# First norm on ScalarE, early up weights and token differences on VectorE alone, in a two-layer hybrid decoder step

## The chip, the cores and the metric

The kernel runs on one core of one Trainium2 chip. The time is the device time of one execution in microseconds, the median over several runs.

## The reference

One inference step of a two-layer decoder for a prompt of 1024 tokens and a sample group of 8 x 8 tokens, 1088 tokens in all, model width 1024, in float32. Layer 0 mixes tokens by two state-space heads, layer 1 by latent attention over a paged cache. Both layers end in the same way; this is what the change touches:

```python
def layer_norm(x, g, b):
    mu = jnp.mean(x, -1, keepdims=True)
    var = jnp.mean(jnp.square(x - mu), -1, keepdims=True)
    return (x - mu) * lax.rsqrt(var + EPS) * g + b

def conv_ffn(x, buf, w_up, conv_w, conv_b, w_down):      # d_ff 2816, both halves 5632 columns
    h = x @ w_up
    h, new_buf = causal_dwconv(h, buf, conv_w, conv_b)   # depthwise, width 3
    return (silu(h[..., :D_FF]) * h[..., D_FF:]) @ w_down, new_buf

x = layer_norm(ALPHA * x + mixer(x), ln1_g, ln1_b)       # mixer ends in an output projection
x = layer_norm(ALPHA * x + conv_ffn(x), ln2_g, ln2_b)
```

## The kernel before

A float32 product is made of three passes of a reduced float format, hi x hi, hi x lo and lo x hi (`mm3`, L207-213). So every operand is split: ScalarE casts it to hi, VectorE subtracts hi from it for lo (`split` L218, `lo` L216, `load_split` L222-226 for weights that come through a raw buffer, where another engine can be named for the subtraction). Tokens lie in nine tiles (eight of 128, one of 64). SBUF is divided by hand into fields A to H whose space passes from one stage to the next. The order of instructions on each engine is set by a scheduler from the program's order and from which buffers are free; a generator's `yield` marks where a caller may put other work.

The stages of a layer, with their place in the trace of layer 0 and of layer 1:

- **Output projection and first norm**, `out_ln` (L1519-1578), 424 to 530 and 2236 to 2322. Two halves of 512 columns. In the second half each finished token tile is added to the residual, normalised by `ln` (L234-246: statistics on VectorE, square root on ScalarE, reciprocal, then two VectorE passes of 128x1024 with the gain and bias rows broadcast over the partitions), stored to `xm` in DRAM, and turned by eight TensorE transposes (`to_raw`, L261-272), which ScalarE copies from PSUM into `XT`, one half of the tokens each.
- **Up-projection**, first part of `ffn` (L276-437), to about 1040 and 2840. 22 blocks of columns. Within one, seven products P1 to P7 in the manner of Strassen stand for eight block products, for each half u of the tokens; a product is 12 matmuls of 272 columns, a block 168. The products need differences of weight quarters (`sums` L326-331 on GpSimd, S4 at L337) and of token quarters (`tokens` L296-315: per half eleven differences and lo parts, 128x1088, at L301, of which three run on GpSimd, and seven casts at L304). Block 0 runs u = 0 first, then u = 1; the raw weights of block 1 go into the space that `XT` leaves.
- **Down-projection**, second part of `ffn` (L439-548), to about 1300 and 3097. Three passes over the tokens (three tiles each), each with 22 steps: `fetch` loads one row block of `w_dn` and the activations of the step, through a ring of two raw weight buffers `wr` and four split ones `wd`. At steps 14 to 16 the residual rows come back from `xm` (`residual` L499-502), after the last step `finish` (L479) adds the products, and `norm` does the second norm in the next pass.
- **Input projection of layer 1**, `in1` (L1605 on), behind the third pass. Its weights come in eight pieces of 128x704 through two raw buffers of their own, split by ScalarE and GpSimd.

Of the kernel before, what the change touches and what calls it, by code (L numbers as in the profile page):

```python
# [113 lines left out]
class Net:  # L114
# [132 lines left out]

    def to_T(self, x, M, x_, c0):
# [12 lines left out]
    def to_raw(self, x, M, XT, c0):  # L261

        nc = self.nc
        for a in range(0, 8, 4):
            t = self.ps("tr")
            for j in range(4):
                nc.tensor.transpose(t[:, j * M : (j + 1) * M], x[:, (a + j) * P : (a + j + 1) * P], self.ident[:M, :M])
            tv = t[:, : 4 * M].rearrange("p (k m) -> p k m", k=4)
            for u in range(2):
                lo, hi = max(c0, u * HT), min(c0 + M, u * HT + HT)  # L270
                if lo < hi:
                    nc.scalar.copy(XT[u][:, a : a + 4, lo - u * HT : hi - u * HT], tv[:, :, lo - c0 : hi - c0])


    def ffn(self, i, XT, gt, src, dst, fields):

        nc, A = self.nc, self.A
        V, G = nc.vector, nc.gpsimd  # L280
        gp, gw, gr, gs, gc, ge, gx = (self.group() for _ in range(7))
        cpar, stt, ffp = gp("F^", 2 * NBLK, 4), gp("F^", 2 * NBLK, NB, 2), gp("F^", 2 * NBLK, 2)
# [4 lines left out]
        X = {}  # L287
        for p, g, fl in (("P1", gc, "C"), ("P6", gc, "C"), ("P2", ge, "E"), *((p, gx, fields) for p in ("P5", "P7", "P4", "P3"))):
            X[p] = [g(fl, 2, 4, QT) for _ in range(2)]
        W = {p: [gs("HEC", 4 * P) for _ in range(2)] for p in PRODUCTS}  # L290
        raws = [gw("F", 2 * D)]
# [4 lines left out]
        def tokens(u):  # L296

            x = XT[u]
            B11, B21 = x[:, :4, :QT], x[:, 4:, :QT]
            B12, B22 = x[:, :4, QT:], x[:, 4:, QT:]  # L300
            sub = lambda eng, o, a, b: eng.tensor_tensor(o, a, b, op=ALU.subtract)  # L301

            def parts(p, full, eng=V):
                nc.scalar.copy(X[p][u][:, 0], full)  # L304
                sub(eng, X[p][u][:, 1], full, X[p][u][:, 0])


            parts("P1", B11)
            parts("P2", B21)
            sub(V, B11, B12, B11)  # L310
            sub(G, B12, B22, B12)
            parts("P3", B22, G)
            sub(V, B22, B22, B11)
            sub(V, B21, B21, B22)
            parts("P6", B22)
            parts("P5", B11)
            parts("P7", B12, G)
            parts("P4", B21)


        def load(blk):
            raw = raws[blk % len(raws)]
            for half in range(2):
                nc.sync.dma_start(raw[:, half * D : half * D + D], A["w_up"][i, half * NBLK + blk])

        def sums(blk):  # L326
            raw = raws[blk % len(raws)]
            A11, A12, A21, A22 = (raw[:, k * 512 : k * 512 + 512] for k in range(4))
# [72 lines left out]
        load(0)  # L401
        sums(0)
        for p in first:
            weights(p)
# [15 lines left out]
        for blk in range(NBLK):  # L420
            if blk + 1 < NBLK:
                load(blk + 1)
# [19 lines left out]
        ar = [gl("F", 384) for _ in range(3)]  # L442
        wr = [gl("F", D) for _ in range(2)]
# [55 lines left out]
        def residual(b, j):  # L499
            t = groups[b][j]  # L500
            M = min(P, NT - t * P)
            nc.sync.dma_start(res[j][:M], src[rows(t), :])
# [9 lines left out]
        x_ = yield  # L512
        self.epoch("H", F32)
        gb = self.load_ln(g, "H", "ln2", i)
        res = [g("HF", D) for _ in range(3)]
        todo = [(b, k) for b in range(3) for k in range(NBLK)]
        late = []
        for n, (b, k) in enumerate(todo):
# [66 lines left out]
def arrange(x):  # L585
# [35 lines left out]
    for k in ("ln1_g", "ln1_b", "ln2_g", "ln2_b"):  # L621
        a[k] = lay(x[k])
    a["w_up"] = lay(x["ffn_w_up"].reshape(2, 8, P, 44, P).transpose(0, 3, 2, 1, 4).reshape(2, 44, P, D))
# [54 lines left out]
class Layer0(Net):  # L678
# [840 lines left out]
    def out_ln(self, name, i, m_, XT, res, src, dst, ks=range(8), rows=None):  # L1519
# [38 lines left out]
        gb = self.load_ln(g, "F^", "ln1", i)  # L1558
        self.epoch("H", F32R)
        xs = self.stack(g("H", 2, 4, P), m_)  # L1560
        for nh in range(2):
            if nh:
                for n in range(8):
                    weights(1, n)
            for tt in self.token_tiles if nh else range(4, NTT):
# [7 lines left out]
                if nh:  # L1573
                    x = res[:M, tt, :]
                    self.ln(x, M, gb, f"a{i}_{tt}")
                    nc.sync.dma_start(dst[tt * P : tt * P + M, :], x)
                    self.to_raw(x, M, XT, tt * P)
# [6 lines left out]
class Layer1(Layer0):  # L1584
# [19 lines left out]
    def in1(self, x_):  # L1604
# [4 lines left out]
        gw = self.group()  # L1609
        raws = [gw("F", 2, 352) for _ in range(2)]  # L1610
# [7 lines left out]
        gw.free()  # L1618
        yield
# [738 lines left out]
    def run(self):  # L2358
# [9 lines left out]
        for _ in self.out_ln("w_out0", 0, m_, XT, res, A["x_tok"], xm[0]):  # L2368
# [5 lines left out]
        xs = self.dp.tile([NT, D], F32, tag="xs", name="xs")  # L2374
        ffn = self.ffn(0, XT, gt, xm[0], xs, "BD")
# [4 lines left out]
        ffn.send(x_)  # L2380
        self.places()
        rest = self.in1(x_)
        next(rest)
# [14 lines left out]
        out = []  # L2398

        def then():  # L2400
# [13 lines left out]
            out.extend((m_, XT, self.out_ln("w_out1", 1, m_, XT, res, xs, xm[1], heads, rows)))  # L2414
# [20 lines left out]
        ffn = self.ffn(1, XT, gd, xm[1], A["o_y"], "AB")  # L2435
        next(ffn)
        ffn.send(None)
# [25 lines left out]
```

## Time and profile before

| | |
|---|---|
| median of 3 runs | 3106.66 us (3103.35 to 3110.38) |
| profiled execution | 3098.84 us, of which the span is 3097.1 us |
| instructions in the span | 51653 |
| mean granted TensorE clock | 0.975 of full speed |
| moved by DMA | 356.32 MB, 115 GB/s on the mean |

The page gives the busy time of each engine over the whole span, which says little of a single stage. For that, the trace is asked in four ways: the waits of an engine, each with the instruction that ended it; windows, that is the busy time of every engine within a stretch, with the granted TensorE clock (1.00 is 2.4 GHz, 0.50 is 1.2 GHz) and the load of the DMA engines; timelines, instruction by instruction; and the issues of DMAs with the time to their landing. Times in a row are microseconds from the span's start.

### The profile page before, as it was taken

How to read it: one execution, taken by the hardware profiler on the slowest of the kernel's cores; microseconds unless marked ns; L12 is line 12 of the kernel's file. 1: busy time of each engine (PE TensorE's matmuls, PEld its weight loads, DVE VectorE, ACT ScalarE, POOL GpSimd, SP SyncE). 2: the span in 40 equal slices, each digit the busy share in tenths (PEclk: the TensorE clock that was granted, in tenths of full speed). 3: DMA queues.
4: the chain of work that ended last, by engine and by line, in shares of the span. 5: the costliest groups of instructions: out<-in, count | busy, mean ns of one | idle time of the engine just before them, and what ended most of it. 6: DMA issues, size and time to landing. Idle time of an engine off the chain costs nothing.

```text
span 3097.1 us, 51653 instructions
## 1 busy us (share of the span) xinstructions
PE 2967.7 (96%) x19503; PEld 2685.6 (87%) x19503; DVE 2370.2 (77%) x4066; ACT 1554.6 (50%) x2733; POOL 1345.9 (43%) x1299
## 2 busy tenths in 40 slices
PE   8999998799999999999999999999996999999998
PEld 7888786799999888798998888888875999999887
DVE  8753647888989666547667999999768988987665
ACT  3434632444444443345555888888524444444432
POOL 2652521666666100101112999989306666662000
PEclk9999899899999999999999999999997999999999
DMA  3223132222222666510103444444621222225664
GB/s 141 73 54 119 52 124 87 71 70 83 77 71 77 205 214 208 157 46 24 32 28 101 167 160 152 170 171 170 207 86 61 81 74 77 81 69 189 215 207 152
DMA packets 145150, 356.32 MB, mean 115 GB/s; under 512 B 27469, under 2 KB 82957, under 8 KB 136709
## 3 DMA queue, kind: packets, MB, share of 16 engines
q1 hardware_dynamic: 133600, 267.99, 27.1%
q0 software_dynamic: 9216, 83.89, 7.6%
q8 instruction: 154, 2.52, 0.3%
q10 hardware_dynamic: 2084, 1.14, 0.1%
q14 instruction: 96, 0.78, 0.1%
HBM read 293.67 MB, written 58.11 MB: 114 GB/s over the span
## 4 chain that ended last, share of the span: by engine, by line
PE 78%; DVE 13%; ACT 4%; DMA 2%; issue 2%; POOL 2%; ACTq 0%; DVEq 0%; SPq 0%; POOLq 0%
PE ps L211 21%; PE ps L213 21%; PE ps L212 21%; DVE fieldH L2221 2%; PE ps L2277 2%; PE ps L2167 2%; DVE fieldD L216 1%; PE ps L2200 1%; PE ps L471 1%; DVE fieldF L2243 1%; DVE fieldB L216 1%; PE ps L1956 1%; PE ps L2181 1%; PE ps L1925 1%; PE ps L1922 1%
## 5 line engine op out<-in xcount | busy, mean ns | idle before, releaser
L212 PE MATMUL ps<-fieldB,fieldE 128*128 128x272 f32 (+4 forms) x960 | 301.1, 314 | 0.1
L211 PE MATMUL ps<-fieldC,fieldE 128*128 128x512 f32 (+2 forms) x740 | 286.3, 387 | 0.0
L213 PE MATMUL ps<-fieldC,fieldE 128*128 128x512 f32 (+2 forms) x740 | 285.9, 386 | 0.0
L212 PE MATMUL ps<-fieldC,fieldE 128*128 128x512 f32 (+2 forms) x740 | 285.7, 386 | 0.0
L216 DVE TENSOR_TENSOR fieldE<-fieldF,fieldE 128x512 fp32r<-128x512 f32 (+4 forms) x265 | 157.1, 608 | 110.7 <-ACT fieldE L456 103.4
L226 DVE TENSOR_TENSOR fieldC<-fieldF,fieldC 128x1024 fp32r<-128x1024 f32 x132 | 162.3, 1230 | 100.5 <-ACT fieldC L225 100.1
L211 PE MATMUL ps<-fieldC,fieldH 128*128 128x272 f32 x704 | 206.5, 293 | 11.8 <-ACT fieldC L304 11.7
L212 PE MATMUL ps<-fieldC,fieldH 128*128 128x272 f32 x704 | 205.0, 291 | 4.9 <-DVE fieldC L301 4.9
L213 PE MATMUL ps<-fieldC,fieldH 128*128 128x272 f32 x704 | 205.3, 292 | 0.0
L225 ACT CAST fieldC<-fieldF 128x1024 fp32r<-128x1024 f32 x132 | 138.5, 1049 | 106.1 <-PE ps L471 56.2
L211 PE MATMUL ps<-fieldA,fieldE 128*128 128x362 f32 (+4 forms) x560 | 180.7, 324 | 7.6 <-ACT fieldA L878 7.3
L212 PEld LDWEIGHTS ps<-fieldB,fieldE 128*128 128x128 f32 x960 | 185.4, 193 | 2.0 <-DVE fieldB L879 0.5
L213 PE MATMUL ps<-fieldA,fieldE 128*128 128x362 f32 (+4 forms) x560 | 182.0, 325 | 0.0
L211 PE MATMUL ps<-fieldB,fieldE 128*128 128x272 f32 (+2 forms) x576 | 171.7, 299 | 2.5 <-DVE fieldD L358 2.5
L213 PE MATMUL ps<-fieldB,fieldE 128*128 128x272 f32 (+2 forms) x576 | 170.6, 296 | 0.0
L213 PEld LDWEIGHTS ps<-fieldC,fieldE 128*128 128x128 f32 x740 | 138.9, 188 | 28.2 <-DVE fieldE L216 0.4
L212 PEld LDWEIGHTS ps<-fieldC,fieldE 128*128 128x128 f32 x740 | 138.8, 188 | 27.4
L211 PEld LDWEIGHTS ps<-fieldC,fieldE 128*128 128x128 f32 x740 | 139.0, 188 | 26.9
L380 DVE SCALAR_TENSOR_TENSOR fieldA<-fieldA,fieldF 128x544 f32<-128x544 f32 (+1 forms) x176 | 145.8, 866 | 21.4 <-ACT fieldA L378 21.4
L380 DVE SCALAR_TENSOR_TENSOR fieldD<-fieldD,fieldF 128x544 f32<-128x544 f32 (+1 forms) x176 | 144.8, 861 | 21.4 <-ACT fieldD L378 21.3
L456 ACT CAST fieldE<-fieldF 128x384 fp32r<-128x384 f32 (+1 forms) x132 | 65.1, 495 | 185.7 <-PE ps L212 160.8
L216 DVE TENSOR_TENSOR fieldD<-ps,fieldE 128x1024 fp32r<-128x1024 f32 x128 | 153.9, 1210 | 1.7 <-ACT fieldE L2171 1.5
(702 smaller groups left out, 10299.7 us busy)
## 6 DMA issues: line engine op xcount, KB each, us to landing
fieldF<-w_dn SPq DMA_DIRECT2D x132, 512.0 KB, 3.6
fieldF<-w_up SPq DMA_DIRECT2D x44, 512.0 KB, 3.6
fieldF<-act SPq DMA_DIRECT2D x88, 192.0 KB, 2.9
fieldA<-w_up SPq DMA_DIRECT2D x22, 512.0 KB, 3.6
fieldD<-w_up SPq DMA_DIRECT2D x22, 512.0 KB, 3.5
fieldF<-w_in SPq DMA_DIRECT2D x16, 512.0 KB, 4.2
fieldF<-w_out SPq DMA_DIRECT2D x32, 256.0 KB, 3.0
xm<-fieldC SPq DMA_DIRECT2D x16, 512.0 KB, 2.6
```

The lines of the kernel that those rows point to most:

```text
L211: mm(out, wh, xh, start=first, stop=False, **kw)
L212: mm(out, wh, xl, start=False, stop=False, **kw)
L213: mm(out, wl, xh, start=False, stop=last, **kw)
L216: self.nc.vector.tensor_tensor(out, full, hi, op=ALU.subtract)
L225: self.nc.scalar.copy(hi, raw)
L226: (eng or self.nc.vector).tensor_tensor(lo, raw, hi, op=ALU.subtract)
L380: V.scalar_tensor_tensor(y[:, :n], x[:, tap : tap + n], c(tap), y[:, :n], op0=ALU.mult, op1=ALU.add)
L456: nc.scalar.copy(a[:, :N], raw)
L471: nc.tensor.matmul(ps, a[:, 256 : 256 + P], w[:, s, cs], start=k + s == 0, stop=k + s == NBLK)
L2167: nc.tensor.transpose(ps[:, t * P : t * P + P], raws[i % 4][:, c : c + P], self.ident)
L2221: V.tensor_tensor_reduce(o, ps[H], o, op0=ALU.add, op1=ALU.max, accum_out=out[H], scale=1.0, scalar=first)
L2277: nc.tensor.matmul(o, x, y, start=t + s == 0, stop=t + s == (8 if J < 8 else 1))
```

## The change

**Norm.** In `out_ln`, `ln` becomes `ln_hat`: the statistics as before, then one VectorE operation on 128x1 and one ScalarE activation over 128x1024 give x̂, the row without gain and bias. x̂ is what `xm` now holds. `to_raw` applies gain and bias where they are per-partition columns, while it copies the transposed blocks: eight activations of 128x128 with scale and bias in place of two copies of 128x512 (columns come from a new small array `ln1_T`). The down-projection's `residual` makes ALPHA·(x̂·g + b) by two VectorE passes, and `finish` adds without a factor. The field with gain and bias rows in the down-projection is loaded anew by `gains`, with ln1 rows at step 12 of each pass and ln2 rows for the second norm.

**Up weights.** `ffn` is a generator whose first part now runs inside `out_ln`, behind the split of the second half's weights: it loads block 0, splits three quarters and makes the four sums on VectorE. The other four products' weights are split behind `out_ln`.

**Token differences.** All 22 are on VectorE.

**Input projection.** The eight weight pieces are loaded at the odd steps 1 to 15 of the third pass of layer 0's down-projection, through `wr`, lo on VectorE.

```diff
+    def ln_hat(self, x, M, tag):
...
+        V.tensor_scalar(mv[:M, 0:1], mv[:M, 0:1], rs[:M], -1.0, op0=ALU.mult, op1=ALU.mult)
+        nc.scalar.activation(x, x, AF.Identity, bias=mv[:M, 0:1], scale=rs[:M])
...
-    def to_raw(self, x, M, XT, c0):
+    def to_raw(self, x, M, XT, c0, gb):
...
-                    nc.scalar.copy(XT[u][:, a : a + 4, lo - u * HT : hi - u * HT], tv[:, :, lo - c0 : hi - c0])
+                        nc.scalar.activation(o, v, AF.Identity, bias=gb[:, 1, k : k + 1], scale=gb[:, 0, k : k + 1])
...
     def ffn(self, i, XT, gt, src, dst, fields):
...
+        raws = [gw("F^", 2 * D)]
+        A11, A12, A21, A22 = load(0)
+        for p, full in (("P1", A11), ("P2", A12), ("P4", A22)):
+            W[p] = [gs("H", 4 * P) for _ in range(2)]
+            self.split(*W[p], full)
+        for o, a, b, op in ((A11, A11, A21, ALU.subtract), (A21, A21, A22, ALU.add), (A22, A22, A11, ALU.subtract), (A12, A12, A22, ALU.subtract)):
+            V.tensor_tensor(o, a, b, op=op)
+        left0 = dict(S1=A21, S2=A22, S3=A11, S4=A12)
+        yield
...
-            sub(G, B12, B22, B12)
-            parts("P3", B22, G)
+            sub(B12, B22, B12)
+            parts("P3", B22)
...
-        load(0)
-        sums(0)
-        for p in first:
-            weights(p)
+        for p in ("P6", "P5", "P7", "P3"):
+            self.split(*W[p], left0[PRODUCTS[p][0]])
         tokens(0)
...
-                V.scalar_tensor_tensor(v, v, ALPHA, ps[:M], op0=ALU.mult, op1=ALU.add)
+                V.tensor_tensor(v, v, ps[:M], op=ALU.add)
...
+            V.scalar_tensor_tensor(x, x, ALPHA, gb[:M, 0], op0=ALU.mult, op1=ALU.mult)
+            V.scalar_tensor_tensor(x, gb[:M, 1], ALPHA, x, op0=ALU.mult, op1=ALU.add)
+
+        def gains(which):
+            for k, n in enumerate("gb"):
+                nc.sync.dma_start(gb[:, k], A[f"{which}_{n}"][i : i + 1, :].partition_broadcast(P))
...
+            if b == 2 and 1 <= k < 17 and k % 2:
+                next(others, None)
+            if b and k == 0:
+                gains("ln2")
+            if k == 12:
+                gains("ln1")
+            if b == 2 and k == 17:
+                gains("ln2")
...
     def out_ln(self, name, i, m_, XT, res, src, dst, early, ks=range(8), rows=None):
...
                 for n in range(8):
                     weights(1, n)
+                early()
...
-                    self.ln(x, M, gb, f"a{i}_{tt}")
+                    self.ln_hat(x, M, f"a{i}_{tt}")
...
-                self.load_split(w[:, 0, ks], w[:, 1, ks], raws[k % 2], A["w_in1"][half][:, ks], nc.gpsimd)
+                self.load_split(w[:, 0, ks], w[:, 1, ks], shaped(self.wr[k % 2][:, :704], 2, 352), A["w_in1"][half][:, ks])
+                yield
```

The instructions move in three places. First VectorE at the last token tile of `out_ln` in layer 0 (names with `bsta_7` and `bmva_7` are its statistics, `fieldC_3709` its rows, L301 before and L342 now the token differences). Before:

```order
L1542 SCALAR_TENSOR_TENSOR fieldC_3709<-fieldC_3709,ps_4391 128x512
L216 TENSOR_TENSOR fieldE_4444<-fieldF_67,fieldE_4444 128x512
L240 BN_STATS bsta_7_4418<-fieldC_3709 128x6
L301 TENSOR_TENSOR fieldE_4444<-fieldA_2594,fieldE_4444 128x1088
L241 BN_AGGR bmva_7_4417<-bsta_7_4418 128x2
L245 SCALAR_TENSOR_TENSOR fieldC_3709<-fieldC_3709,bmva_7_4417,fieldF_67 128x1024
L244 RECIPROCAL brsa_7_4422<-brsa_7_4422 128x1
L301 TENSOR_TENSOR fieldE_4444<-fieldA_2594,fieldE_4444 128x1088
L246 SCALAR_TENSOR_TENSOR fieldC_3709<-fieldC_3709,brsa_7_4422,fieldF_67 128x1024
L216 TENSOR_TENSOR fieldH_3847<-fieldF_67,fieldH_3847 128x512 x2
```

Changed:

```order
L1590 SCALAR_TENSOR_TENSOR fieldC_3709<-fieldC_3709,ps_4457 128x512
L255 BN_STATS bsta_7_4484<-fieldC_3709 128x6
L216 TENSOR_TENSOR fieldE_4516<-fieldF_67,fieldE_4516 128x512
L256 BN_AGGR bmva_7_4483<-bsta_7_4484 128x2
L216 TENSOR_TENSOR fieldE_4516<-fieldF_67,fieldE_4516 128x512
L259 RECIPROCAL brsa_7_4488<-brsa_7_4488 128x1
L216 TENSOR_TENSOR fieldE_4516<-fieldF_67,fieldE_4516 128x512
L260 TENSOR_SCALAR bmva_7_4483<-bmva_7_4483,brsa_7_4488 128x1
L342 TENSOR_TENSOR fieldE_4516<-fieldA_2594,fieldE_4516 128x1088 x2
L342 TENSOR_TENSOR fieldA_2594<-fieldA_2594 128x4x272
L342 TENSOR_TENSOR fieldD_4520<-fieldA_2594,fieldD_4520 128x1088
```

The two passes of 128x1024 are gone, splits of up weights stand between the small steps of the norm, and token differences follow on one another.

Second GpSimd in the same place. Before (L329 to L337 are the sums of block 0, L301 the token differences):

```order
L301 TENSOR_TENSOR fieldD_4449<-fieldA_2594,fieldD_4449 128x1088
L329 TENSOR_TENSOR fieldF_67<-fieldF_67 128x512
L330 TENSOR_TENSOR fieldF_67<-fieldF_67 128x512
L331 TENSOR_TENSOR fieldF_67<-fieldF_67 128x512
L337 TENSOR_TENSOR fieldF_67<-fieldF_67 128x512
L294 MEMSET fieldF_67 128x88
L301 TENSOR_TENSOR fieldD_4449<-fieldA_2594,fieldD_4449 128x1088
L301 TENSOR_TENSOR fieldA_2594<-fieldA_2594 128x4x272 x2
L301 TENSOR_TENSOR fieldB_4448<-fieldA_2594,fieldB_4448 128x1088
```

Changed (L363 is the first sum of block 1):

```order
L335 MEMSET fieldF_67 128x88
L444 MEMSET fieldA_2594 128x2 x2
L420 COPY fieldA_2594<-fieldF_67 128x8x2 x2
L416 COPY fieldA_2594<-fieldA_2594 128x2 x2
L418 COPY fieldF_67<-fieldA_2594 128x2
L421 COPY fieldA_2594<-fieldA_2594 128x8x8
L425 COPY fieldF_67<-fieldA_2594 128x16
L428 TENSOR_TENSOR fieldA_2594<-fieldA_2594 128x544
L418 COPY fieldF_67<-fieldA_2594 128x2
L421 COPY fieldA_2594<-fieldA_2594 128x8x8
L425 COPY fieldF_67<-fieldA_2594 128x16
L363 TENSOR_TENSOR fieldF_67<-fieldA_2594 128x512
```

Only small copies, and the gate of the convolution, are left on GpSimd ahead of block 1.

Third SP's queue in the third pass of layer 0's down-projection. Before, the pieces of the input projection (printed `w_in`) come behind the last `w_dn`:

```order
L224 DMA fieldF_67<-w_dn 128x1024
L454 DMA fieldF_67<-act_4451 128x384
L224 DMA fieldF_67<-w_dn 128x1024
L224 DMA fieldF_67<-w_in 128x704 x5
L495 DMA xs<-fieldH_9877 128x1024
L224 DMA fieldF_67<-w_in 128x704 x3
```

Changed, a part of the pass (L526 stores second-norm rows, L534 loads x̂ rows, L541 gain rows):

```order
L224 DMA fieldF_67<-w_in 128x704
L485 DMA fieldF_67<-act_4522 128x384
L526 DMA xs<-fieldH_9936 128x1024
L541 DMA fieldH_9936<-ln_g 128x1024
L224 DMA fieldF_67<-w_dn 128x1024 x2
L485 DMA fieldF_67<-act_4522 128x384 x2
L526 DMA xs<-fieldH_9936 128x1024
L224 DMA fieldF_67<-w_in 128x704
L541 DMA fieldH_9936<-ln_b 128x1024
L224 DMA fieldF_67<-w_dn 128x1024
```

Between two pieces there are two `w_dn` blocks, all through the same two raw buffers.

## Rows read from the trace of the kernel before

**Rows 1.** The page: busy time, share of the span and instructions of each engine.
```profile
PE 2967.7 (96%) x19503; PEld 2685.6 (87%) x19503; DVE 2370.2 (77%) x4066; ACT 1554.6 (50%) x2733; POOL 1345.9 (43%) x1299
```

**Rows 2.** Waits of TensorE: line, releaser, us in total, times, longest.
```profile
PE ps L267 <- DVE fieldC L246: 19.7, 2, 10.3
PE ps L211 <- ACT fieldC L304: 11.7, 2, 6.2
PE ps L212 <- DVE fieldB L301: 4.4, 1, 4.4
```

**Rows 3.** Windows: us; PE, PEld, DVE, ACT, POOL busy (x); clock; DMA share; GB/s.
```profile
490.00:530.00 40.00, 39.99 (x201) 32.21 (x199) 29.36 (x43) 9.46 (x23) 0.00 (x0) 1.00 0.26 98
530.00:542.00 12.00, 1.75 (x9) 1.57 (x8) 10.03 (x9) 5.05 (x7) 7.80 (x4) 0.59 0.09 35
542.00:564.00 22.00, 5.34 (x18) 3.85 (x17) 16.89 (x11) 10.60 (x12) 14.36 (x10) 0.50 0.23 73
564.00:570.00 6.00, 6.00 (x29) 5.85 (x29) 6.00 (x4) 1.64 (x2) 3.08 (x1) 0.53 0.01 3
570.00:584.50 14.50, 14.50 (x118) 14.50 (x117) 13.03 (x17) 5.84 (x10) 5.12 (x6) 1.00 0.21 73
2322.00:2379.00 57.00, 27.12 (x168) 24.84 (x168) 50.41 (x42) 23.77 (x32) 32.98 (x21) 0.70 0.16 54
```

**Rows 4.** Timeline of TensorE: start, us, line, operation, [idle before, releaser].
```profile
587.39 0.39 PE L211 MATMUL ps<-fieldD,fieldE 128*128 128x272 f32 x1 [2.51 <-DVE fieldA L358]
```

**Rows 5.** Timeline of VectorE, around the first boundary and in the down-projection.
```profile
533.42 3.27 DVE L245 SCALAR_TENSOR_TENSOR fieldC<-fieldC,bmva,fieldF 128x1024 f32<-128x1024 f32 x1
559.91 3.58 DVE L301 TENSOR_TENSOR fieldB<-fieldA,fieldB 128x1088 fp32r<-128x1088 f32 x1
569.35 1.28 DVE L301 TENSOR_TENSOR fieldD<-fieldA,fieldD 128x1088 fp32r<-128x1088 f32 x1
571.75 0.43 DVE L358 TENSOR_TENSOR fieldA<-fieldA,ps 128x272 f32<-128x272 f32 x1
575.07 1.29 DVE L301 TENSOR_TENSOR fieldD<-fieldA,fieldD 128x1088 fp32r<-128x1088 f32 x1
...
1271.46 1.23 DVE L226 TENSOR_TENSOR fieldC<-fieldF,fieldC 128x1024 fp32r<-128x1024 f32 x1 [0.40 <-ACT fieldC L225]
1275.54 1.22 DVE L226 TENSOR_TENSOR fieldC<-fieldF,fieldC 128x1024 fp32r<-128x1024 f32 x1 [0.39 <-ACT fieldC L225]
```

**Rows 6.** Timeline of GpSimd, first boundary.
```profile
536.77 2.30 POOL L329 TENSOR_TENSOR fieldF<-fieldF 128x512 f32<-128x512 f32 x1 [1.16 <-DVE brsa L244]
552.93 5.92 POOL L301 TENSOR_TENSOR fieldA<-fieldA 128x1088 f32<-128x1088 f32 x2 [3.63 <-DVE fieldA L301]
581.48 1.55 POOL L329 TENSOR_TENSOR fieldF<-fieldA 128x512 f32<-128x512 f32 x1 [1.21 <-DMA fieldA<-w_up]
```

**Rows 7.** Timeline of ScalarE, first boundary and down-projection.
```profile
515.62 1.20 ACT L272 COPY fieldA<-ps 128x128 f32<-128x128 f32 x4 [3.19 <-PE ps L267]
...
580.38 1.13 ACT L219 CAST fieldH<-fieldA 128x512 fp32r<-128x512 f32 x2
...
1270.38 1.05 ACT L225 CAST fieldC<-fieldF 128x1024 fp32r<-128x1024 f32 x1
```

**Rows 8.** Timeline of SP's queue, first boundary.
```profile
576.50 0.81 SPq L324 DMA_DIRECT2D fieldA<-w_up  x2
```

**Rows 9.** Windows, the stretch in which the input projection of layer 1 begins.
```profile
1300.00:1316.00 16.00, 8.76 (x37) 6.93 (x36) 7.87 (x12) 4.76 (x9) 6.99 (x5) 0.72 0.49 161
```

**Rows 10.** DMA issues, 1160 to 1200 and 1200 to 1235: KB, us to landing.
```profile
fieldF<-w_dn SPq DMA_DIRECT2D x9, 512.0 KB, 3.5
...
fieldF<-w_dn SPq DMA_DIRECT2D x9, 512.0 KB, 4.3
xs<-fieldH SPq DMA_DIRECT2D x2, 512.0 KB, 5.7
```

**Rows 11.** Windows, the down-projection of layer 0.
```profile
1040.00:1285.00 245.00, 244.81 (x1106) 202.81 (x1105) 147.75 (x210) 99.59 (x147) 2.48 (x2) 1.00 0.65 204
```

More of the change, by code (lines that the diff above doesn't have):

```diff
@@ L246, in ln @@
         V.scalar_tensor_tensor(x, x, rs[:M], gb[:M, 1, :], op0=ALU.mult, op1=ALU.add)
+    def ln_hat(self, x, M, tag):
+        nc = self.nc
+        V = nc.vector
+        mv = self.sm.tile([P, 2], F32, tag="bmv", name="bmv" + tag)
+        st = self.sm.tile([P, 2, 6], F32, tag="bst", name="bst" + tag)
+        for k in range(2):
+            V.bn_stats(st[:M, k, :], x[:, k * 512 : k * 512 + 512])
+        V.bn_aggr(mv[:M], st[:M])
+        rs = self.sm.tile([P, 1], F32, tag="brs", name="brs" + tag)
+        nc.scalar.activation(rs[:M], mv[:M, 1:2], AF.Sqrt, bias=self.eps[:M])
+        V.reciprocal(rs[:M], rs[:M])
+        V.tensor_scalar(mv[:M, 0:1], mv[:M, 0:1], rs[:M], -1.0, op0=ALU.mult, op1=ALU.mult)
+        nc.scalar.activation(x, x, AF.Identity, bias=mv[:M, 0:1], scale=rs[:M])
     def to_T(self, x, M, x_, c0):
@@ L281, in ffn, with load @@
         gp, gw, gr, gs, gc, ge, gx = (self.group() for _ in range(7))
-        cpar, stt, ffp = gp("F^", 2 * NBLK, 4), gp("F^", 2 * NBLK, NB, 2), gp("F^", 2 * NBLK, 2)
+        X, W = {}, {}
+        def load(blk):
+            raw = raws[blk % len(raws)]
+            for half in range(2):
+                nc.sync.dma_start(raw[:, half * D : half * D + D], A["w_up"][i, half * NBLK + blk])
+            return [raw[:, k * 512 : k * 512 + 512] for k in range(4)]
+        raws = [gw("F^", 2 * D)]
[7 more added lines that the diff above has]
+        yield
+        cpar, stt, ffp = gp("F", 2 * NBLK, 4), gp("F", 2 * NBLK, NB, 2), gp("F", 2 * NBLK, 2)
         nc.sync.dma_start(cpar, A["ffn_cp"][i])
@@ L286, in ffn @@
             self.epoch(x, F32R)
[L287 to L291, printed above, removed]
+        X = {p: [] for p in PRODUCTS}
+        for u in range(2):
+            for p in ("P1", "P2"):
+                X[p].append((ge, gc)[u]("EC"[u], 2, 4, QT))
+        for p in ("P6", "P5", "P7", "P4", "P3"):
+            for u in range(2):
+                X[p].append(gc("C", 2, 4, QT) if p == "P6" else gx(fields, 2, 4, QT))
+        for p in ("P6", "P5", "P7", "P3"):
+            W[p] = [gs("HE", 4 * P) for _ in range(2)]
         S = [gw("F", 512) for _ in range(2)]
@@ L300, in tokens, with parts @@
             B12, B22 = x[:, :4, QT:], x[:, 4:, QT:]
-            sub = lambda eng, o, a, b: eng.tensor_tensor(o, a, b, op=ALU.subtract)
-            def parts(p, full, eng=V):
+            sub = lambda o, a, b: V.tensor_tensor(o, a, b, op=ALU.subtract)
+            def parts(p, full):
                 nc.scalar.copy(X[p][u][:, 0], full)
-                sub(eng, X[p][u][:, 1], full, X[p][u][:, 0])
+                sub(X[p][u][:, 1], full, X[p][u][:, 0])
             parts("P1", B11)
             parts("P2", B21)
-            sub(V, B11, B12, B11)
-            sub(G, B12, B22, B12)
-            parts("P3", B22, G)
-            sub(V, B22, B22, B11)
-            sub(V, B21, B21, B22)
+            sub(B11, B12, B11)
+            sub(B12, B22, B12)
+            parts("P3", B22)
+            sub(B22, B22, B11)
             parts("P6", B22)
             parts("P5", B11)
-            parts("P7", B12, G)
+            parts("P7", B12)
+            sub(B21, B21, B22)
             parts("P4", B21)
[L321 to L324, printed above, removed]
         def sums(blk):
-            raw = raws[blk % len(raws)]
-            A11, A12, A21, A22 = (raw[:, k * 512 : k * 512 + 512] for k in range(4))
+            A11, A12, A21, A22 = load(blk)
             G.tensor_tensor(S[0], A11, A21, op=ALU.subtract)
@@ L400, in ffn @@
         first = ("P1", "P2", "P6", "P5", "P7", "P4", "P3")
[L401 to L404 removed]
+        for p in ("P6", "P5", "P7", "P3"):
+            self.split(*W[p], left0[PRODUCTS[p][0]])
         tokens(0)
@@ L441, in ffn @@
         ah = [g("E", 768) for _ in range(3)]
-        ar = [gl("F", 384) for _ in range(3)]
-        wr = [gl("F", D) for _ in range(2)]
+        ar = [gl("F^", 384) for _ in range(3)]
+        wr = [gl("F^", D) for _ in range(2)]
         groups = ((0, 1, 8), (2, 3, 4), (5, 6, 7))
@@ L1516, in mix0, with out_ln @@
         return [self.m0, m1]
-    def out_ln(self, name, i, m_, XT, res, src, dst, ks=range(8), rows=None):
+    def out_ln(self, name, i, m_, XT, res, src, dst, early, ks=range(8), rows=None):
         nc, A = self.nc, self.A
@@ L2367, in run @@
         self.first = [self.ps() for _ in range(4)]
-        for _ in self.out_ln("w_out0", 0, m_, XT, res, A["x_tok"], xm[0]):
+        xs = self.dp.tile([NT, D], F32, tag="xs", name="xs")
+        ffn = self.ffn(0, XT, gt, xm[0], xs, "BD")
+        for _ in self.out_ln("w_out0", 0, m_, XT, res, A["x_tok"], xm[0], lambda: next(ffn)):
             pass
@@ L2397, in run @@
         heads = range(8)
-        out = []
+        out, ffn1 = [], []
         def then():
@@ L2412, in rows @@
                 self.load_split(hi, lo, raws[n % 2], self.Od[h])
-            out.extend((m_, XT, self.out_ln("w_out1", 1, m_, XT, res, xs, xm[1], heads, rows)))
+            out.extend((m_, XT, self.out_ln("w_out1", 1, m_, XT, res, xs, xm[1], lambda: next(ffn1[0]), heads, rows)))
+            ffn1.append(self.ffn(1, XT, gd, xm[1], A["o_y"], "AB"))
             t = [self.ps("wide") for _ in range(2)]
```

43 lines of the change are left out of this document (20 added, 23 removed).

## The prediction

> **What bounds the kernel now.** I began with the page: TensorE is busy for 96% of the span [rows 1], so a gain must come out of the stretches in which it stands still. The waits of TensorE, sorted by length, say where these are [rows 2]. The longest is L267, the transposes of the first norm, waiting for the second VectorE pass of `ln` (19.7 us in two waits). Next are the first products of the up-projection, waiting for the casts of the token operands (L304) and for their differences (L301). All of these lie at one kind of place, where the output projection ends and the up-projection starts, once per layer. The windows show it in one piece [rows 3]: up to 530 TensorE is full at clock 1.00; then it works 1.75 of 12 us, 5.34 of 22, and only from 564 on without gaps. The granted clock falls meanwhile to 0.50 (1.2 GHz) and is back at 1.00 (2.4 GHz) after 570, behind 6 us of unbroken matmuls. Layer 1 has the same stretch, 27.12 us of work in 57.
>
> Who sets the pace there is seen in the timeline of VectorE [rows 5]. It does the norm (the first pass alone 3.27 us), then the token differences: 1.28 us each, one per 1.20 us, when GpSimd is idle (569.35), 3.58 us when GpSimd works on the same fields (559.91). The last one ends at 576.36; TensorE gets the last product of block 0 at 587.39 [rows 4]. GpSimd, in the same stretch, makes the sums of block 0 (2.30 us the first) and six of the token differences (two in 5.92 us) [rows 6].
>
> The third place is the input projection of layer 1: TensorE works 8.76 of 16 us behind the last down-projection pass, at clock 0.72, because its weights are only then loaded and split [rows 9].
>
> **The first norm.** Removed on VectorE are two passes of 128x1024, 3.27 us the one that has a row [rows 5]. In their place come a 128x1 operation and, on ScalarE, one 128x1024 activation, which I price as the cast of that size, 1.05 us [rows 7]. Four ScalarE copies of 128x128 took 1.20 us together [rows 7], so the eight scaled copies cost about 2.4 us a tile. ScalarE has room: 50% busy over the span [rows 1]. Within the output projection TensorE is full (39.99 of 40 us [rows 3]), so the earlier tiles gain nothing; only the last tile does. In the kernel before, VectorE starts the last tile's first norm pass at 533.42 with one token difference already made; now it makes two splits more and that difference not, and is through with the statistics at about 533.6, ready for tokens.
>
> **The token differences.** All 22 are now on VectorE, with nothing on GpSimd beside them: 22 x 1.20 = 26.4 us. In the new order six adds of products stand among them, some 0.35 us each (0.43 with its fixed part [rows 5]), and two convolution taps, which I take at 0.7. That is 26.4 + 2.1 + 1.4 = 29.9 us: the last difference ends at 533.6 + 29.9 = 563.5, where before it was 576.36, so 12.9 us earlier. Bounds: at 1.28 each the end is 565.3; should the scaled copies and casts of ScalarE pace the start by 3 us, 566.5.
>
> **Block 1.** Its weights go to the space that the tokens leave, so the load still starts behind the last difference: before, issued at 576.50 [rows 8], cast at 580.38 [rows 7], GpSimd's first sum at 581.48, and three sums of about 1.6 us stand ahead of the second product [rows 6]. Now: issue 563.6, cast 567.5, sums from 568.6 to 573.5, second product (P6) at about 574.5. Before, TensorE at 587.39 still owed 12 matmuls of block 0 and 12 of block 1's P1, 24 x 0.123 us (118 in 14.50 us [rows 3]) = 3.0, so its P6 came at 590.4. The gain is 590.4 - 574.5 = **15.9 us**, 16 with layer 1's boundary alike: **32 for both**. TensorE has to do block 0's 168 matmuls by 568: at 1.2 GHz they alone take 37 us (29 in 6.00 us at 0.53 [rows 3] is 0.22 each at 0.50), at full clock 21. I take it that the clock rises in time, since at the low clock TensorE falls behind VectorE's pace and so works without gaps, and after such a stretch it rose before. Ends of one boundary: 10 and 22 us, the upper if the load, not paced by sums, lets P2 and others fill in.
>
> **Block 0's weights.** Loaded, split and summed earlier, under the second half of the output projection, where VectorE has 29.36 of 40 us busy [rows 3]: four sums and three splits, some 6 us of VectorE, fit into the idle 10. If they come ahead of a split that TensorE waits for, they cost 0 to 1 us a layer; I take 0.5 for both.
>
> **The input projection's weights.** They now come in the third pass of the down-projection of layer 0. Gained: the idle 16.00 - 8.76 = 7.2 us [rows 9], and, of 8.76 us at mean clock 0.72, about 3 (0.56 of the stretch at half speed, evenly spread 2.5; more if the work fell there): **10 us**. Against it stands the ring: these pieces use the down-projection's own two raw buffers. A buffer is held from the load's issue till VectorE has split it. The load takes 3.5 us, beside stores 4.3 [rows 10], the cast 1.05 [rows 7] and the split 1.23 [rows 5]: 5.8 or 6.6 us. A 704-column piece, at 704/1024 of the 2.3, takes 5.1 or 5.9. Two steps need two weights and one piece in two buffers: (2 x 5.8 + 5.1) / 2 = 8.35 us, or 9.55, and TensorE uses up two steps in 8.16 (splits at 1271.46 and 1275.54 [rows 5]). Over eight pieces that is 1.5 or 11 us too slow. The split buffers, four, are ahead by one to two steps, 4 to 8 us; I take 6. So 0 or 5 us of stall. The DMA engines are 0.65 busy there at 204 GB/s [rows 11]; 2.9 MB of pieces and some 3 MB of gain rows within about 75 us add 80 GB/s, 0.25 of share, so I stand near the upper end: **4 us lost**, ends 0 and 12. Net: 6.
>
> A rule bears on this term. The rows give a 512 KB weight 3.5 to 4.3 us from issue to landing [rows 10]. The Trainium skill, "DMA: Bandwidth & Descriptors", section "Anatomy of one DMA — SWDGE (gpsimd) path", fits a transfer by a fixed 2.0 us and its bytes at 436 GB/s, for the path that GpSimd issues. An estimate by it is 3.2 us for a weight and 2.8 for a piece, and two steps would take 7.7 us, under 8.16: no stall, 10 net, and 3064 in place of 3068. The trace is above it already without the pieces, so I stay with the rows.
>
> **Added in the down-projection.** Each token tile takes two passes of 128x1024 on VectorE, 18 a layer at about 1.3 us, and the final addition loses its multiplication. VectorE is busy 147.75 of 245 us there [rows 11], and the tile is needed 5 steps (20 us) later: hidden, price 0. Uncovered it would be 2.6 us a tile. The gain rows, read six times a layer with 1 MB in place of once, lie on the SP queue between weight loads; hidden in the first two passes, counted in the third.
>
> **Sum.** 32 + 6 + 0 - 0.5 is about 38 us off. Against the profiled execution (3098.84 us, span 3097.1) this makes 3061; that execution is 7.8 us below the median of the runs shown, so from 3106.66 I forecast **3068**.
>
> **The rivals.**
> *The clock stays low through block 0.* Against it: the return to 1.00 after 564. For it: between 542 and 564 matmuls came in short groups and the clock was 0.50 throughout [rows 3], and the new token rate still feeds TensorE in groups. Then block 0 takes 37 us from about 541 with 2 us of waits, to 580, where before it ended at 587.39 + 1.5 = 588.9 with 12 matmuls of block 1 done: 6.5 to 7 us per boundary, so 13 + 6 - 0.5 = 19 off, **3087**. Chance 0.15.
> *The ring starves.* With loads of 5 to 6 us two steps take 10.6 to 12.1 us, and eight pieces lose 20 to 32 less 6: 14 to 26 in place of 4, **3078 to 3090**. For it: 0.9 DMA share; against: 3.5 us at 0.61 to 4.3 at 0.71 is a mild slope. Chance 0.18.
> *Slower than before.* The same ring, but with loads beyond 7.4 us: (2 x 9.7 + 9.0) / 2 = 14.2 us for two steps, 48 lost over eight pieces, 42 after the lead, which is all of 32 + 10. At 8 us the time is about **3114**. It needs loads of twice their length in rows 10 through the whole third pass. Chance 0.04.
> *No change.* The last token difference was not what TensorE waited for: another chain, such as the store of the last x rows that must leave field C before operands go there, sets the start in both. For it: L211 waits name ScalarE's casts, not VectorE [rows 2]. Against: these casts wait for VectorE's work in their turn. Within 6 us of 3107; chance 0.05.
>
> **How the numbers follow.** The likeliest case has 0.58, with its own range 3050 to 3080. A measurement of this kernel tells some 0.2% (6 us) from no change. All but the last two rivals are faster by more: 0.58 + 0.15 + 0.18 = 0.91; same 0.05; slower 0.04. The low end takes 22 us per boundary and 12 net in the input projection, 56 off, and 4 us for the spread of runs (3103.35 to 3110.38): 3046. The high end takes the first two rivals nearly together: 13 + 0 off, 3094.
>
> **What would show it.** Right: the wait of L267 on VectorE is gone or below 5 us; the last L342 ends some 33 us behind the last matmul of the output projection (46 before); GpSimd has no tensor operation there until block 1's sums; TensorE works unbroken about 45 us behind that matmul; the input projection's L1638 waits are gone, and a few waits of L211 for the weight casts appear in the third pass. Wrong: matmuls of block 0 still 0.22 us apart after that point (first rival); waits for w_dn loads above 10 us together (the ring); or a wait of L267 for ScalarE that takes the place of VectorE's.

## The result, and the profile after

| | before | changed |
|---|---|---|
| median | 3108.52 us (4 runs) | 3074.9 us (4 runs, 3068.33 to 3078.3) |
| ratio | | 0.9892, interval 0.987 to 0.9913 |
| span of the profiled execution | 3097.1 us | 3073.9 us |

The spans differ by 23.2 us only, the medians by 33.6, and the windows of a stage that the change does not touch say why: same window, before and then changed.

```profile
110.00:140.00 30.00, 25.10 (x158) 22.83 (x158) 24.85 (x39) 12.24 (x21) 20.25 (x18) 0.94 0.29 74
```

```profile
110.00:140.00 30.00, 24.77 (x124) 21.66 (x123) 20.56 (x34) 10.00 (x18) 18.28 (x16) 0.72 0.29 74
```

The order of the instructions on every compute engine is the same up to the output projection of layer 0, but in this execution the clock was at 1.2 GHz for longer (0.72 against 0.94), and that projection began 8.7 us later (432.74 against 424.01). In the thirteen profiled executions of the changed kernel and its edits it began at 427.1 to 434.1, so up to 7 us of this is spread between executions; 424.0 lies outside that range, and whether all of the 8.7 is spread is not shown. So from here on stages are compared by their length between two events of TensorE, which holds this out. The columns: end of the last token difference behind the last matmul of the output projection; from that matmul to the down-projection (to its first matmul on the short token tile, the 13th of all); the down-projection of layer 0 from there, to the last step of the first pass + the rest, up to the first matmul of the input projection; the input projection, to its last transposes in the first stage. With two numbers: layer 0 / layer 1.

| run | last difference | to down-projection | down-projection | input projection |
|---|---|---|---|---|
| before | 46.3 / 45.9 | 506.2 / 507.3 | 76.2 + 187.2 | 94.4 |
| changed | 33.8 / 33.0 | 492.0 / 491.8 | 77.3 + 195.4 | 82.1 |
| changed, again (e12) | 33.9 / 32.9 | 492.1 / 491.1 | 77.8 + 196.2 | 81.9 |
| e1 pieces back | 33.9 / 32.9 | 492.2 / 491.3 | 77.0 + 186.6 | 92.3 |
| e2 GpSimd tokens | 41.8 / 39.3 | 500.7 / 498.2 | 77.8 + 196.4 | 82.0 |
| e3 no early part | 33.9 / 32.9 | 492.6 / 491.2 | 77.9 + 194.6 | 81.9 |
| e4 old norm | 40.5 / 40.9 | 498.8 / 499.6 | 76.2 + 193.8 | 82.0 |
| e5 rows once | 33.9 / 33.1 | 492.1 / 491.8 | 76.5 + 191.1 | 82.0 |
| e6 own buffer | 33.9 / 33.0 | 492.1 / 491.7 | 80.8 + 189.0 | 82.0 |
| e7 spread | 33.8 / 32.8 | 492.0 / 491.1 | 85.3 + 195.5 | 82.1 |
| e8 P2 second | 33.9 / 33.5 | 492.1 / 492.6 | 78.0 + 193.9 | 82.4 |
| e9 every third | 33.9 / 33.0 | 492.1 / 491.7 | 77.6 + 186.7 | 81.9 |
| e10 deferred casts | 34.0 / 33.6 | 490.4 / 490.1 | 77.8 + 193.2 | 82.0 |
| e11 e9 and e10 | 33.9 / 32.8 | 490.4 / 489.4 | 77.0 + 187.4 | 82.0 |

The boundaries, as the stretch of the second column is called here, gave 14.2 + 15.5 = 29.7 us and the input projection 12.3; the down-projection of layer 0 lost 9.3, that of layer 1 1.6 in its first pass. That is 31.1 us together, beside 33.6 in the medians. What lies between these stages is the same within 2 us. The waits of TensorE (total, times, longest) show the exchange: the 19.7 us for L246 [rows 2] are gone, and the longest of the new ones are

```profile
PE ps L211 <- ACT fieldH L219: 8.6, 4, 3.1
...
PE ps L282 <- ACT fieldC L261: 3.9, 1, 3.9
PE ps L211 <- ACT fieldE L345: 3.7, 1, 3.7
...
PE ps L211 <- ACT fieldC L225: 2.8, 2, 2.7
```

the weight casts of block 1, the new norm's pass (layer 1), the first token casts, and the weight casts of the third down-projection pass. The windows of the first boundary, which answer to [rows 3], of the third pass, and of a short stretch in it:

```profile
537.70:571.60 33.90, 24.05 (x155) 22.42 (x154) 33.70 (x39) 25.50 (x37) 2.83 (x6) 0.90 0.14 47
577.60:592.00 14.40, 10.46 (x69) 10.02 (x69) 13.95 (x16) 6.40 (x13) 12.32 (x9) 0.88 0.25 73
1204.00:1303.00 99.00, 93.88 (x418) 76.03 (x417) 69.97 (x92) 38.27 (x58) 0.00 (x0) 0.98 0.68 219
1256.40:1259.80 3.40, 2.85 (x7) 2.27 (x8) 3.40 (x5) 1.41 (x3) 0.00 (x0) 0.50 0.87 285
```

At the boundary VectorE is busy without a gap (33.70 of 33.90), GpSimd almost idle, and TensorE works 24.05 us at clock 0.90 where it worked some 7 us in 34 at 0.50 to 0.59. In the third pass TensorE stands still for 5.1 us (99.00 - 93.88); behind the longest of these waits, which ends at 1255.7, its clock is at 0.50 for 3.4 us. The timeline of VectorE at the boundary, for [rows 5]:

```profile
541.10 0.21 DVE L260 TENSOR_SCALAR bmva<-bmva,brsa 128x1 f32<-128x1 f32 x1
541.37 2.49 DVE L342 TENSOR_TENSOR fieldE<-fieldA,fieldE 128x1088 fp32r<-128x1088 f32 x2
...
570.24 1.28 DVE L342 TENSOR_TENSOR fieldD<-fieldA,fieldD 128x1088 fp32r<-128x1088 f32 x1
```

No difference takes 3.58 us any more; the last matmul ends at 537.73, the last difference at 571.52.

### The profile page after: what moved, and what is told of

Read it like the earlier page. It is cut to its first block, busy times and chain, and to the rows that moved or that the text cites. A ratio compares the mean times of both kernels' runs of the same rounds, so it can differ in the third digit from the quotient of the medians.

```text
span 3073.9 us, 51795 instructions
## 1 busy us (share of the span) xinstructions
PE 2977.1 (97%) x19503; PEld 2689.1 (87%) x19503; DVE 2368.7 (77%) x4112; ACT 1614.6 (53%) x2871; POOL 1279.5 (42%) x1271
## 4 chain that ended last, share of the span: by engine, by line
PE 71%; DVE 14%; DMA 5%; ACT 4%; issue 4%; POOL 1%; SPq 0%; ACTq 0%; POOLq 0%; DVEq 0%
PE ps L213 18%; PE ps L211 18%; PE ps L212 18%; DMA fieldF<-w_dn 3%; DVE fieldH L2268 2%; PE ps L2324 2%; PE ps L2214 2%; PE ps L2247 1%; DVE fieldD L216 1%; DVE fieldF L2290 1%; DVE fieldB L216 1%; PE ps L2003 1%; PE ps L2228 1%; DVE fieldC L226 1%; ACT fieldC L225 1%
## 5 line engine op out<-in xcount | busy, mean ns | idle before, releaser
L211 PE MATMUL ps<-fieldA,fieldE 128*128 128x272 f32 (+3 forms) x736 | 233.3, 318 | 9.2 <-ACT fieldA L926 7.3
L213 PE MATMUL ps<-fieldA,fieldE 128*128 128x272 f32 (+3 forms) x736 | 233.7, 318 | 0.0
L216 DVE TENSOR_TENSOR fieldE<-fieldF,fieldE 128x512 fp32r<-128x512 f32 (+4 forms) x265 | 137.5, 534 | 58.3 <-ACT fieldE L487 44.8
L211 PEld LDWEIGHTS ps<-fieldA,fieldE 128*128 128x128 f32 x736 | 142.2, 193 | 10.5 <-ACT fieldA L926 7.3
```

What stands on the lines that cost most here:

```text
L211: mm(out, wh, xh, start=first, stop=False, **kw)
L213: mm(out, wl, xh, start=False, stop=last, **kw)
L216: self.nc.vector.tensor_tensor(out, full, hi, op=ALU.subtract)
```

## The experiments

All are edits of the changed kernel. Ratios are to the kernel before, in the same comparison.

**e1, pieces of the input projection back.** The load loop has its own `raws`, GpSimd and one `yield` again, and the down-projection's `next(others, None)` goes.

> Only the input projection's weights go back behind the third pass, with two raw buffers of their own and lo parts on GpSimd; all else is as in the changed kernel (3074.9 us median). Theory: the move won 12.3 us at the start of the input projection and lost 9.4 in the third pass of the down-projection, so it is nearly even; undone, the down-projection of layer 0 takes about 264 us again in place of 272.7 (first matmul of it to first of the input projection), the input projection 94 in place of 82, and the kernel is 2 to 4 us slower, about 3078. Rival (as forecast): only 4 us were lost to the ring, the rest of the 9.4 comes from the gain rows, which stay; then the down-projection keeps some 268 us and the kernel is 6 to 8 us slower, about 3082.

Measured: 3076.16 us, ratio 0.9915 (0.9895 to 0.9935). The ratios' intervals overlap, so the table decides: down-projection 263.6, input projection 92.3, together 355.9 against 354.8. The third pass alone, from its first matmul to the input projection's first, takes 93.3 us here and 101.7 in the changed kernel. Without the pieces neither the second nor the third pass has a stall although the gain rows stay, so the theory holds and the rival falls; the move was worth 1 us.

**e2, six token differences on GpSimd.**

```diff
-            sub(B12, B22, B12)
-            parts("P3", B22)
+            sub(B12, B22, B12, G)
+            parts("P3", B22, G)
...
-            parts("P7", B12)
+            parts("P7", B12, G)
```

> Only the six token differences per layer that ran on GpSimd before go back there. Theory: VectorE paces the boundary and GpSimd's share slows it instead of helping: each of the six takes 2.5 to 3 us on GpSimd and stretches VectorE's own from 1.2 to 3.6 us, so the last difference ends 6 to 8 us later behind the last matmul of the output projection (33.8 now, 40 to 42 then), and the kernel is 12 to 16 us slower, about 3089. Rival: six operations less on VectorE (7.2 us) outweigh the contention, the last difference ends no later, and the time is within 4 us of 3075.

Measured: 3090.97 us, 0.9953 (0.9939 to 0.9967). The last difference ends 8.0 and 6.3 us later, the boundaries are 8.7 and 6.4 longer, 15.1 in all. The timelines of VectorE and GpSimd of this run show how.

```profile
551.73 2.62 DVE L342 TENSOR_TENSOR fieldA<-fieldA 128x1088 f32<-128x1088 f32 x2 [4.84 <-POOL fieldA L342]
...
555.46 1.28 DVE L342 TENSOR_TENSOR fieldC<-fieldA,fieldC 128x1088 fp32r<-128x1088 f32 x1
556.67 3.61 DVE L342 TENSOR_TENSOR fieldD<-fieldA,fieldD 128x1088 fp32r<-128x1088 f32 x1
...
555.70 3.43 POOL L342 TENSOR_TENSOR fieldB<-fieldA,fieldB 128x1088 fp32r<-128x1088 f32 x1
```

Two things act in layer 0. VectorE's own operations are stretched: same operation, same shape, 1.28 and 3.61 us, three times in this boundary, 7.0 us. And VectorE waits for GpSimd's results, 4.84 us here and 1.40 once more. Together this is 13.2 us, against the 7.2 that six operations less save. The Trainium skill, "SBUF — State Buffer", section "Who interferes with whom", states that two inputs in SBUF make a VectorE operation contend with a GpSimd one that reads SBUF, and that the ports they share are locked by one of them at a time. The trace agrees: the long operation began inside GpSimd's (555.70 to 559.13) and ended 1.15 us behind it, which is about its own length.

**e3, no early weights.** `early` does nothing; the first part of `ffn` is written behind `out_ln`.

> Only the early part goes: block 0's up weights are loaded, split and summed behind the output projection, sums still on VectorE. Theory: seven splits and four sums, about 0.65 us each, then stand on VectorE beside the token differences, four sums and three splits more than now: up to 4.5 us per boundary, the kernel 5 to 9 us slower, about 3082. Rival: TensorE waits for block 1's sums on GpSimd anyway (3.1 us in one wait at P6 of block 1), and VectorE has the room: within 3 us of 3075.

Measured: 3075.35 us, 0.9904 (0.9888 to 0.9921), no stage changed. But the edit did not make the weights late: its timeline has the four sums (L316) from 446.02 on, 12.2 us behind the start of the output projection, as in the changed kernel, whose rows these are:

```profile
444.98 0.68 DVE L316 TENSOR_TENSOR fieldF<-fieldF 128x512 f32<-128x512 f32 x1
...
447.38 2.13 DVE L316 TENSOR_TENSOR fieldF<-fieldF 128x512 f32<-128x512 f32 x3
```

The scheduler starts this part at the same place either way, so where it is written costs nothing, and the run says nothing of what early weights are worth.

**e4, the first norm on VectorE.** e3, with `ln`, plain copies, no passes in `residual`, `finish` with its factor and no `gains` but once, as before.

> As the run without early weights, and the first norm is the old one on VectorE too (two passes of 128x1024 with broadcast rows, plain copies of the transposes, no residual passes in the down-projection, second-norm rows loaded once). Theory: 5.5 us more of VectorE per boundary behind the last matmul, and the rows of gain and bias hold the space that block 0's weights need until the norm is over, so the boundary is 8 to 11 us longer than in the run without early weights; against it the down-projection of layer 0 loses the gain rows: its third pass waits less, 4 us back. Net 14 to 18 us slower than the run without early weights, about 3098. Rival: the norm's passes are hidden beside the casts of ScalarE; then it is no slower than the run without early weights, or faster by the 4 us.

Measured: 3085.04 us, 0.9934 (0.9917 to 0.995), 10 us slower than e3 where 14 to 18 were expected. Against e3 the boundaries are 6.2 and 8.4 us longer, 14.6; the down-projection is 2.5 shorter, but its third pass still stalls (100.4 us, of which 4.3 are waits). Two rows, of VectorE and of SP's queue:

```profile
543.74 1.27 DVE L245 SCALAR_TENSOR_TENSOR fieldC<-fieldC,bmva,fieldF 128x1024 f32<-128x1024 f32 x1
...
545.03 0.33 SPq L304 DMA_DIRECT2D fieldF<-w_up  x1
```

With GpSimd idle a norm pass takes 1.27 us, not 3.27 [rows 5]; two of them are 2.5. The rest comes from the space: block 0's weights are loaded at 545.03, when the gain rows leave field F, so all seven splits and four sums stand between the token differences, four splits and four sums (8 x 0.60 = 4.8 us) more than in e3. The losses of e2 and e4, 15.1 + 14.6 = 29.7, add up to what the boundaries won.

**e5, gain rows once; e6, an own raw buffer as well.** Both compute another y, as their expectations say.

```diff
-            if b and k == 0:
-                gains("ln2")
-            if k == 12:
+            if n == 12:
                 gains("ln1")
-            if b == 2 and k == 17:
-                gains("ln2")
...
-        self.wr = wr
+        self.wr = [gl("F", 704)]
```

> The rows of gain and bias in the down-projection are loaded once per layer in place of six times; the second norm and the later residual rows then use the first norm's rows, so y is another function, with the same work on every engine. Theory: the third pass of layer 0's down-projection is slow because eight pieces pass through its two raw buffers, and the rows are the smaller part: the down-projection takes about 270 us (272.7 in the changed kernel, 270.0 with the old norm, 263.6 with the pieces taken out), and its first pass loses the extra 1.1 to 1.6 us in both layers. Rival: the load on the DMA engines is what slows it; without the rows it takes 264 to 266.

> As the run with the rows loaded once, and one row serves for gain and bias (so y is again another function), which frees space for a raw buffer of 704 columns that belongs to the pieces of the input projection alone; they no longer pass through the two buffers of the down-projection. Theory (buffers): the down-projection of layer 0 is down to 263 to 265 us with the pieces still loaded in its third pass, the input projection stays at 82. Rival (DMA load): it stays within 1 us of the run with the rows loaded once.

Measured, one execution each. In six runs with the same down-projection (the changed kernel, e12, e2, e3, e8, e10) the third pass takes 99.8 to 103.0 us, with 3.8 to 5.3 us of TensorE's waits. In e5 it takes 97.7 with 2.9 of waits, in e6 93.3, as without the pieces in e1. There TensorE has no wait left (window of 89 us):

```profile
1205.00:1294.00 89.00, 89.00 (x406) 73.95 (x405) 61.46 (x82) 31.39 (x48) 0.00 (x0) 1.00 0.59 190
```

So the shared buffers are what starves the ring: with a buffer of their own, the same pieces at the same steps cost the third pass nothing in this one execution. What the gain rows add is open: 2 to 5 us by e5, nothing by e4, which loads its rows once too. Fewer rows did not make a weight land sooner (median 4.3 us in e5's third pass, 4.1 in the changed kernel's), only a piece (3.1 against 4.6). The totals do not show any of this: e6's first pass was 4 us long for no cause in the edit, and its second 2.3; the first was 76.2 to 82.2 us in runs with the same code, in either layer. So e6's 270 in place of the expected 264 says nothing, and neither does e5's first pass (76.5 in layer 0, 80.4 in layer 1).

**e7, pieces spread over all passes.** `if n in range(3, 51, 6)`.

> The eight pieces are loaded one in six steps over all three passes (steps 3, 9, ... 45 of 66), not at every second step of the third. Through two buffers six steps then need (6 x 5.8 + 5.1) / 2 = 20 us, with 24.5 to use up. Theory: no step waits for weights, the down-projection of layer 0 takes 264 to 266 us, the input projection 82, and the kernel is 6 to 9 us faster than the changed one, about 3067. Rival: a piece costs some 1.1 us wherever it stands; 271 to 273 and 3075.

Measured: 3081.69 us, 0.9922 (0.9896 to 0.9948), and a down-projection of 280.8 us against 272.7: the theory fell. The first pass took 85.3 us. Its steps are shorter (two of its three tiles are full, 3.6 us a step), which leaves less room; how much of the 9 us the pieces cost is not shown, since in layer 1 of this run, without pieces, the pass took 82.2. The rest of the loss lies at the start of the second pass, where TensorE waits for the additions of `finish`. These stand on VectorE behind splits whose loads are late, one of which waits 2.2 us for ScalarE's cast.

**e9, pieces at every third step of the second and third pass.** `if b and k in (1, 4, 7, 10)`.

> The eight pieces stand at steps 1, 4, 7 and 10 of the second and of the third pass, one in three steps, ahead of the loads of first-norm rows and of x rows at steps 12 to 16. Two buffers then need (3 x 5.8 + 5.1) / 2 = 11.3 us for three steps, with 12.2 to use up. Theory (buffers): the stalls of the third pass (9 us in the changed kernel) go, the second and third pass of layer 0's down-projection take 188 to 190 us together in place of 195.4 (187.2 before), the input projection stays at 82, and the kernel is 5 to 7 us faster than the changed one, about 3068. Rival: the start of the second and of the third pass, where rows are read back and gain rows are loaded, has no room for a piece; the stall moves there (as in the run that spread them over all passes), 194 to 196.

Measured: 3065.2 us, 0.9878 (0.9854 to 0.9903). The two passes take 186.7 us, as before the change, and the input projection keeps its 81.9. The third pass:

```profile
1200.00:1290.00 90.00, 90.00 (x413) 74.77 (x412) 65.63 (x86) 34.38 (x52) 0.00 (x0) 1.00 0.69 225
```

TensorE never waits, at a DMA share of 0.69, no less than the 0.68 at which it starved, so the share does not tell whether the ring holds. The edit changed two things: a piece at every third step and not every second, and none beside the row loads of steps 12 to 17, where the stalls of the changed kernel begin (TensorE first waits at step 12 of 0 to 21). Which of the two did it is not told apart.

**e8, P2 second in block 1.** `PRODUCTS if blk > 1 else first`.

> Block 1 takes its products in the order of block 0 (P1, P2, P6, ...), so that P2, whose weights need no sum, fills the 3.1 us in which TensorE waits for P6's weights. Theory: the wait goes, and the low clock after it (0.60 to 0.80 for 5 us): 3 to 4 us per layer, from the last matmul of the output projection to the down-projection 488 to 489 us in place of 492, the kernel 6 to 8 us faster, about 3068. Rival: the sums for P5 and P7 come as late, the wait moves behind P6, and 492 stays.

Measured: 3070.89 us, 0.9898 (0.987 to 0.9925), boundaries 492.1 and 492.6: nothing won, though not as the rival had it. TensorE still runs P6 behind P1, after 2.94 us of waiting, and P2 behind it from 580.64. ScalarE's timeline of this run shows what holds P2:

```profile
575.87 0.62 ACT L219 CAST fieldE<-fieldA 128x512 fp32r<-128x512 f32 x1 [1.03 <-POOL fieldA L364]
577.54 0.62 ACT L219 CAST fieldH<-fieldF 128x512 fp32r<-128x512 f32 x1 [1.05 <-POOL fieldF L365]
...
579.75 0.66 ACT L394 COPY fieldA<-ps 128x272 f32<-128x272 f32 x2
```

P2 adds into P1's bank and must wait till L394 has copied that; the copy stands on ScalarE behind casts that wait for GpSimd's sums, as it does in the changed kernel.

**e10, the four casts deferred.** e8, and behind P2 of block 1:

```diff
...
+                if blk == 1 and p == "P6":
+                    for q in ("P6", "P5", "P7", "P3"):
+                        weights(q)
+                    sums(2)
...
```

> Block 1's products in the order of block 0 (P2 second), and the casts of its four weights that need sums are written behind its first two products, so that on ScalarE fewer of them, which wait for GpSimd, stand ahead of the PSUM copies of P1 that P2 needs. Theory: TensorE's wait behind P1 of block 1 (2.9 to 3.1 us) is ScalarE's order, not the sums as such; it falls below 1.5 us, the boundaries take 489 to 491 us in place of 492.0 and 491.8, 2 to 6 us in all, about 3071. Rival: the sums of GpSimd bound it in any order: 492 in both.

Measured: 3072.21 us, 0.99 (0.9877 to 0.9923); boundaries 490.4 and 490.1, 1.6 and 1.7 less than the changed kernel's (in layer 1 runs with its order took 491.1 to 491.8). The wait is split and shorter, its longest part now 1.56 us and for the copy itself:

```profile
577.36 0.39 PE L211 MATMUL ps<-fieldE,fieldH 128*128 128x272 f32 x1 [1.56 <-ACT fieldA L394]
```

**e11, e9 and e10 together; e12, the changed kernel again.**

> Pieces of the input projection at every third step of the second and third pass, and block 1's casts deferred. Theory: both edits act in different stages and add up, 8.5 us in the down-projection of layer 0 and 1.7 at each boundary: 12 us faster than the changed kernel in the same comparison, 0.984 to 0.987 of the kernel before. Rival: the earlier start of the following stage shifts stores and loads onto one another and the gain of one is lost; then it is within 3 us of the run with every third step alone (0.9878).

> The changed kernel itself, beside the combined one on the same chip. Theory: 0.987 to 0.9913 of the kernel before, as measured first, and 9 to 14 us slower than the combined one. Rival: no difference from the combined one beyond 4 us.

Measured: 3063.19 us, 0.9861 (0.984 to 0.9883), and 3075.01 us, 0.9902 (0.9886 to 0.9918): 12 us apart. The version with both beats both kernels.

## Why the prediction was right

3068 was forecast, 3074.9 measured: faster, inside the range and the likeliest case's own. By its steps:

- **Token differences and norm.** 33.5 us from the last matmul to the last difference were forecast, 33.8 and 33.0 measured; P6 of block 1 at 44.5 us behind, 44.8 measured (582.48). This was the chain that decided, as e2 and e4 show by undoing it. The price of the norm pass was the contended 3.27 us; e4 shows 1.27, and the missing part in the weights that the gain rows kept out. ScalarE's price came from a row read wrongly: of the four copies of [rows 7] two are 128x384, the row names the form of the first. The eight scaled copies took 2.9 us, not 2.4, the norm's activation 1.24, not 1.05; the chain came out within 0.3 us even so. One of the signs named for "wrong" came in part: in layer 1 a transpose waits 3.9 us for ScalarE's norm pass (L261), where it waited 9.4 for VectorE's.
- **The boundary**, 15.9 us forecast, 14.2 and 15.5 measured. Behind the wait for P6 the clock fell: 0.88 on the mean of 577.6 to 592 is 3.5 us at half speed, up to 1.7 us of work lost.
- **The clock rival** fell: 0.90 over the stretch in which block 0 runs, where it had been 0.50.
- **Early weights**, 0.5 us: 0 (the output projection took 105.0 us, 106.0 before), and the scheduler makes them early unasked.
- **The input projection's weights** is the term that was mis-sized: net 6 forecast, 3 by the traces and 1 by e1. The gain was 12.3, not 10; the step "4 us lost" was 9. Its landings were near the upper bound (4.1 us for a weight, 4.6 for a piece, below), which gives (2 x 6.4 + 6.2) / 2 = 9.5 us for two steps, 1.3 too slow, 11 over eight pieces. Less the lead of 6 that is 5, and 5.1 us of waits is what the third pass has. But that pass is 8.4 us longer than in e1 (101.7 against 93.3): the sum put what follows a wait at nothing. The 3.4 us at clock 0.50 behind the first wait make 1.7 of the missing 3; where the rest lies is open, and the lead itself was not measured. The DMA issues of the third pass:

```profile
fieldF<-w_dn SPq DMA_DIRECT2D x18, 512.0 KB, 4.1
...
fieldF<-w_in SPq DMA_DIRECT2D x7, 352.0 KB, 4.6
...
fieldH<-ln_b SPq DMA_DIRECT2D x2, 512.0 KB, 6.9
```

The estimate by the Trainium skill's fit ("DMA: Bandwidth & Descriptors", section "Anatomy of one DMA — SWDGE (gpsimd) path") was 2.8 us for a piece and no stall; the fit is for another issuing path, and the rows, with 4.6 us, decide against it here.

- **Residual passes**, 0: outside the stalls of layer 0's third pass the later passes are unchanged. The first took 77.3 and 77.8 us, 76.2 before, which lies within the spread of that pass in runs with the same code (76.2 to 82.2).

## What to carry to other kernels

Work given to GpSimd as relief can stretch the engine that it relieves: compare the duration of one operation with and without the neighbour before counting a share as saved. Loads that are moved under another stage go through that stage's buffers; count how long each buffer is held per step and place the loads so that the sum stays below the step, rather than trusting an average DMA share. Small constants in place of broadcast rows also free space, which can start the next stage's loads earlier than any edit to the order.

## What the runs showed of the hardware beyond that

The same order of instructions on the compute engines took 427.1 us in one execution and 434.1 in another up to the output projection, with the granted clock different in stretches where TensorE had gaps. In six of the thirteen executions of the changed kernel and its edits it was at 0.50 for 17 us from about 120 on, and the projection began at 432.7 to 434.1; in the other seven it was so for 3.4 us, and the projection began at 427.1 to 428.6. And a row of 1024 values broadcast to 128 partitions took 5.7 and 6.9 us to land, where a plain weight block of the same 512 KB took 4.1 in the same pass; but blocks of x rows took 4.6 there and 6.8 in e9, so that the broadcast is the reason is not shown.
